# Tying a mixing's steps, two sets' copies and the casts at an entry to other rows of W

## The chip, the cores and the metric

The kernel runs on one core of one Trainium2 chip. The metric is the device time of one execution in microseconds; a kernel's time is the median of its timed runs. For the kernel before there are three: 2227.27, 2230.98 and 2233.45 us.

The core's engines run side by side, each through a queue of its own in order: TensorE (PE in the profile; PEld is its weight load), VectorE (DVE), ScalarE (ACT), GpSimd (POOL) and SyncE (SP), which issues transfers. ScalarE and GpSimd issue transfers too; those stand in their queues like any other instruction (ACTq, POOLq).

## The reference

Two layers on 512 tokens of 2048 channels, all in fp32. The first has an attention with forgetting and an RWKV part between the projections `ab_w_in` and `ab_w_out`. The second is a gMLP: `c_w_in` gives u, v and g, and the tokens are mixed in chunks of 128:

```
def chunked_spatial_gating(u, v, ln_g, ln_b, w_s, b_s):
    B, T, _ = v.shape
    u = jax.nn.gelu(u, approximate=False)
    v = layer_norm(jax.nn.gelu(v, approximate=False), ln_g, ln_b)
    vc = v.reshape(B, T // GMLP_CHUNK, GMLP_CHUNK, GMLP_GROUPS, GMLP_GROUP_CH)
    causal = jnp.tril(jnp.ones((GMLP_CHUNK, GMLP_CHUNK), w_s.dtype))
    mixed = jnp.einsum('gts,bnsgc->bntgc', w_s * causal, vc) + b_s.T[:, :, None]
    return u * mixed.reshape(B, T, GMLP_W)
...
        if i % 2 == 0:
            ...
            y = jnp.concatenate([oa * jax.nn.silu(ga), ob * jax.nn.silu(gb)], axis=-1) @ ab_w_out[j]
        else:
            proj = xn @ c_w_in[j]
            u, v, g = _split(proj, (GMLP_W, GMLP_W, GMLP_W))
            oc = chunked_spatial_gating(u, v, c_ln_g[j], c_ln_b[j], c_w_s[j], c_b_s[j])
            y = (oc * jax.nn.silu(g)) @ c_w_out[j]
        h = h + rms_norm(y, norm_post[i])
        h = h + (p[i] @ ple_w_proj[i]) * jax.nn.sigmoid(h @ ple_w_gate[i])
```

There are 16 mixing groups of 128 channels, each with its own 128 x 128 matrix.

## The kernel before

**Rows of W.** Each fp32 operand is split into a high part (ScalarE casts it to a rounded fp32, `whi`, L1544) and the rest (VectorE subtracts, `wlo`, L1545), and a product is three matmuls. The big products behind the first layer's gates (out projection, gate of the per-layer input, `c_w_in`, `c_w_out`, second gate) are each done by seven block products in place of eight (`seven`). Their weights come in pieces of 512 KB, two rows of 128 x 512 each; six of the eight piece buffers are `rq0` to `rq5`, two are `raw`. SyncE loads a piece (L1488), GpSimd's transfers (L1492) or VectorE (L1496) add a second block to it where a product needs a sum. For each row ScalarE casts, VectorE subtracts, and TensorE runs six matmuls of 512 columns, or twelve of 256 (L1580). Four `whi`/`wlo` buffers, and `half` at each fifth row, let the casts run about four rows ahead of TensorE.

**What sets the order.** Everything else is queued with `later(n, step)` on a clock that ticks once a row of W; a scheduler then lays the instructions into each engine's queue by priority, casts and subtracts of W first. `tc.issue_after(x)` binds an instruction to stand behind x in the queue of its engine; it adds no wait.

**The mixing.** In `layer_c`, `mix(g, at)` does one of the 16 groups, eight while the first half of u and g is computed and eight in the second. Its steps: load the saved v (`sq<-vd`, 256 KB, L1659), the group's matrix (L1660) and the two columns of the norm (L1661, L1662) over ScalarE's queue; normalise with four activations (L1668); mask the matrix on GpSimd (L1671); multiply and add the columns on VectorE (L1672, L1673); transpose the matrix on TensorE (L1678); split matrix and values (casts L1680 and L1683, subtracts L1681 and L1684); three matmuls (L1689 to L1691); and combine with u (L1693). The steps are queued at 11 and 4 rows ahead of `at`, at it, and 7 behind, with `at = 40 + int(6.8 * e)` for the e-th of eight.

**The sets.** A set is a block of the activations, or a sum of blocks, split into high and low parts by `finish` (cast L973, subtract L974). In `first_gate`, `early` makes the first set of the second layer and `x2` another.

**The entry.** In `layer_ab` the attention's last gate product is copied out of TensorE's accumulator, half by ScalarE (L2015) and half by VectorE (L2016), and the first rows of the out projection follow.

Of the kernel before, what the change touches and what calls it, by code (L numbers as in the profile page):

```python
# [16 lines left out]
P = 128  # L17
T = 512
# [88 lines left out]
class Net:  # L107
# [862 lines left out]
    def finish(self, src, hi, lo):  # L970

        nc = self.nc
        nc.scalar.copy(hi, src)  # L973
        nc.vector.tensor_tensor(lo, src, f(hi), ALU.subtract)  # L974

# [27 lines left out]
    def run(self):  # L1003
        tc = self.tc
        with ExitStack() as ctx:
# [14 lines left out]
            self.turns = 0  # L1020
            self.clock, self.todo = 0, []
# [7 lines left out]
    def rest(self, cp):  # L1029
        nc, tc, i = self.nc, self.tc, self.i  # L1030
        with ExitStack() as ctx:
# [5 lines left out]
            self.raws = deque([(self.wraw, "raw", 2)] * 2 + [(wq, f"rq{j}", 1) for j in range(6)])  # L1037
# [56 lines left out]
    def first_gate(self, H, state, wp, ps):  # L1094
# [38 lines left out]
        def early(q):  # L1133
            if q == 0:
                cs[1] = self.whole_set()
            self.put(cs[1], q, H[q, 0])

# [10 lines left out]
        steps += [(108 + q, lambda q=q: x2(q)) for q in range(4)]  # L1148
# [328 lines left out]
    def pieces(self, pr, prod, keep):  # L1477
# [20 lines left out]
        for j in range(4):  # L1498
# [36 lines left out]
            for a in range(2):  # L1535
# [5 lines left out]
                else:  # L1541
                    hi, lo = (self.t(self.wq, [P, T], f"half{x}", F32R) for x in range(2))
                with self.tc.high_priority(self.wpri):
                    self.cast = nc.scalar.copy(hi, src)  # L1544
                    nc.vector.tensor_tensor(lo, src, f(hi), ALU.subtract)  # L1545
# [70 lines left out]
    def layer_c(self, cp, sets, steps, accq, after, wp, ps):  # L1616
# [30 lines left out]
        def mix(g, at):  # L1647
# [6 lines left out]
            def load():  # L1654
                par = self.t(wp, [P, T], "accq", bufs=1) if g % 2 else self.rstdB
                own["ws"], own["bc"] = par[:, 0:P], par[:, P : 3 * P].rearrange("p (a c) -> p a c", c=P)
                vn = own["vn"] = self.t(wp, [P, 4, P], "sq")
                with tc.issue_after(self.cast.ins):
                    nc.scalar.dma_start(vn, self.vd[:, g])  # L1659
                nc.scalar.dma_start(own["ws"], i["c_w_s"][0, g])  # L1660
                nc.scalar.dma_start(own["bc"][:, 0, :], i["c_ln_g"][0, gs].partition_broadcast(P))  # L1661
                nc.scalar.dma_start(own["bc"][:, 1, :], i["c_ln_b"][0, gs].partition_broadcast(P))  # L1662

            def norm():
                ws, bc, vn = own["ws"], own["bc"], own["vn"]
                row = lambda j: bc[:, j : j + 1, :].broadcast_to([P, 4, P])
                for m in range(4):
                    nc.scalar.activation(  # L1668
                        vn[:, m, :], vn[:, m, :], AF.Identity, bias=nb[:, m : m + 1], scale=rv[:, m : m + 1]
                    )  # L1670
                nc.gpsimd.affine_select(ws, ws, [[-1, P]], ALU.is_ge, 0.0, 0, 1)  # L1671
                nc.vector.tensor_tensor(vn, vn, row(0), ALU.mult)  # L1672
                nc.vector.tensor_tensor(vn, vn, row(1), ALU.add)  # L1673

            def split():
                vn = own["vn"]
# [372 lines left out]
```

## Time and profile before

| | |
|---|---|
| timed runs | 2227.27, 2230.98, 2233.45 us |
| the profiled execution | 2223.7 us, its span 2222.0 us, mean granted clock 0.998 |
| TensorE busy | 2185.6 us, 98% |
| VectorE, ScalarE, GpSimd busy | 1659.4, 1353.2, 301.9 us |
| transfers | 343 MB, 155 GB/s on average |

The profile is of one execution. Times in its rows are microseconds from the span's start. A row of the timeline gives start, duration, engine, line, operation, what is written from what, the shape, and in brackets how long the engine had been idle and what ended that. A line that starts with an issuing queue (SPq, ACTq) is the issue of a transfer, not its duration. The end of a matmul is modelled, so a matmul ahead of a stop shows longer than it runs.

### The profile page before, as it was taken

Reading aid. Unit: us, or ns where it says so; the run is one execution under the profiler, and the core shown is the slowest. Engines: PE = TensorE matmul, PEld = TensorE weight load, DVE = VectorE, ACT = ScalarE, POOL = GpSimd, SP = SyncE. Lnnn points to the kernel's source line nnn. Section 1 sums busy time; section 2 is a strip of 40 time slices with the busy share of each in tenths; the row PEclk is TensorE's granted clock in tenths of the full one; section 3 lists DMA queues with packets and bytes.
Section 4 is the critical chain, followed back from the end, with each engine's and each line's share of the span. In section 5 each row is a group of like instructions: output and inputs, shape, how many; then the busy total and the mean of one; then the engine's idle time right before and its main releaser. Section 6 shows DMA issues by size and latency. Waiting matters only on the chain.

```text
span 2222.0 us, 43469 instructions
## 1 busy us (share of the span) xinstructions
PE 2185.6 (98%) x16535; PEld 1872.1 (84%) x16535; DVE 1659.4 (75%) x3228; ACT 1353.2 (61%) x2764; POOL 301.9 (14%) x360
## 2 busy tenths in 40 slices
PE   9999999999999999999999999999999999999998
PEld 7878888888888788889999999788877878999887
DVE  8756667657633778886979978987677678978977
ACT  5545545554543677775667766756655567657754
POOL 2001010101000000000210121110221221120031
PEclk9999999999999999999999999999999999999999
DMA  7322322223233633326797888787877887688796
GB/s 238 93 79 58 89 77 80 70 64 91 68 92 99 212 96 98 102 81 204 162 216 241 218 201 221 179 214 202 192 162 206 181 189 176 148 200 264 207 243 169
DMA packets 304144, 343.34 MB, mean 155 GB/s; under 512 B 15758, under 2 KB 187951, under 8 KB 302911
## 3 DMA queue, kind: packets, MB, share of 16 engines
q1 hardware_dynamic: 237438, 240.93, 34.6%
q0 software_dynamic: 44608, 85.99, 22.4%
q10 hardware_dynamic: 21888, 13.64, 2.1%
q8 instruction: 130, 2.13, 0.4%
q14 instruction: 80, 0.65, 0.1%
HBM read 305.61 MB, written 34.90 MB: 153 GB/s over the span
## 4 chain that ended last, share of the span: by engine, by line
PE 79%; DVE 8%; DMA 6%; ACT 4%; issue 2%; ACTq 0%; DVEq 0%; SPq 0%; POOLq 0%
PE mm L1580 37%; PE mm L213 10%; PE mm L215 9%; PE mm L214 9%; DMA sq<-vd 3%; DVE wlo L1545 2%; PE tm L551 1%; DMA rq<-in_ple_w_gate_dram 1%; PE tm L572 1%; ACT whi L1544 1%; PE g L923 1%; PE pp L340 1%; PE tm L484 1%; PE tm L910 1%; PE ch L636 1%
## 5 line engine op out<-in xcount | busy, mean ns | idle before, releaser
L1545 DVE TENSOR_TENSOR wlo<-rq,whi 128x512 fp32r<-128x512 f32 x485 | 329.7, 687 | 118.0 <-ACT whi L1544 115.6
L213 PE MATMUL mm<-xh,whi 128*128 128x512 f32 x992 | 411.7, 415 | 0.0
L1544 ACT CAST whi<-rq 128x512 fp32r<-128x512 f32 x485 | 297.4, 620 | 186.3 <-PE mm L1580 120.1
L215 PE MATMUL mm<-xh,wlo 128*128 128x512 f32 x992 | 391.7, 395 | 0.0
L214 PE MATMUL mm<-xl,whi 128*128 128x512 f32 x992 | 389.6, 393 | 0.0
L197 ACT CAST whi<-raw 128x512 fp32r<-128x512 f32 x272 | 167.5, 617 | 151.4 <-PE mm L214 107.8
L199 DVE TENSOR_TENSOR wlo<-raw,whi 128x512 fp32r<-128x512 f32 x272 | 185.9, 695 | 93.3 <-ACT whi L197 69.6
L215 PEld LDWEIGHTS mm<-xh,wlo 128*128 128x128 f32 x992 | 186.2, 188 | 41.2
L213 PEld LDWEIGHTS mm<-xh,whi 128*128 128x128 f32 x992 | 186.8, 188 | 33.2
L214 PEld LDWEIGHTS mm<-xl,whi 128*128 128x128 f32 x992 | 187.2, 189 | 29.8
L1580 PE MATMUL mm<-whi,yh 128*128 128x512 f32 x424 | 138.9, 394 | 5.1 <-ACT whi L1544 5.1
L1580 PE MATMUL mm<-whi,xl 128*128 128x512 f32 x424 | 137.5, 392 | 1.8 <-ACT whi L1544 0.9
L1580 PE MATMUL mm<-whi,yl 128*128 128x512 f32 x420 | 137.8, 394 | 0.0
L1544 ACT CAST whi<-raw 128x512 fp32r<-128x512 f32 x154 | 94.9, 620 | 69.0 <-PE mm L1580 48.5
L1545 DVE TENSOR_TENSOR wlo<-raw,whi 128x512 fp32r<-128x512 f32 x154 | 104.8, 687 | 39.6 <-ACT whi L1544 39.1
L1580 PE MATMUL mm<-xh,whi 128*128 128x256 f32 x696 | 126.9, 283 | 0.0
L1580 PEld LDWEIGHTS mm<-xh,whi 128*128 128x128 f32 x696 | 108.7, 192 | 0.1
L1492 POOL DMA_DIRECT2D rq<-in_c_w_in_dram x56 | 67.5, 1214 | 274.6 <-DVE wlo L1545 194.9
L1545 DVE TENSOR_TENSOR half<-rq,half 128x512 fp32r<-128x512 f32 x111 | 76.2, 686 | 36.8 <-ACT half L1544 36.6
L1580 PEld LDWEIGHTS mm<-whi,yh 128*128 128x128 f32 x424 | 80.3, 189 | 23.3 <-ACT whi L1544 6.8
L1580 PE MATMUL mm<-xh,wlo 128*128 128x256 f32 x348 | 98.5, 283 | 0.0
L1544 ACT CAST half<-rq 128x512 fp32r<-128x512 f32 x111 | 68.8, 620 | 46.0 <-PE mm L1580 26.9
(531 smaller groups left out, 5187.3 us busy)
## 6 DMA issues: line engine op xcount, KB each, us to landing
raw<-in_ab_w_in_dram SPq DMA_DIRECT2D x128, 512.0 KB, 3.9
rq<-in_c_w_in_dram POOLq DMA_DIRECT2D x56, 512.0 KB, 7.6
rq<-in_c_w_in_dram SPq DMA_DIRECT2D x50, 512.0 KB, 5.2
rq<-in_ple_w_gate_dram SPq DMA_DIRECT2D x44, 512.0 KB, 6.1
rq<-in_ple_w_gate_dram POOLq DMA_DIRECT2D x36, 512.0 KB, 9.4
raw<-in_c_w_in_dram SPq DMA_DIRECT2D x26, 512.0 KB, 7.4
rq<-in_c_w_out_dram SPq DMA_DIRECT2D x24, 512.0 KB, 4.7
rq<-in_ab_w_out_dram POOLq DMA_DIRECT2D x20, 512.0 KB, 7.5
```

Source lines behind the costliest of these rows:

```text
L197: nc.scalar.copy(hi[:, : m * n], src)
L199: self.weng.tensor_tensor(lo[:, : m * n], src, f(hi[:, : m * n]), ALU.subtract)
L213: nc.tensor.matmul(acc, hi, xhi[k], start=(k == 0), stop=False)
L214: nc.tensor.matmul(acc, hi, xlo[k], start=False, stop=False)
L215: nc.tensor.matmul(acc, lo, xhi[k], start=False, stop=(k == nk - 1))
L340: nc.tensor.matmul(acc, mat, part, start=(j == 0), stop=(j == 1))
L484: nc.tensor.matmul(pg[q][:, e], BK[pp, e].rearrange("p a t -> p (a t)"), AR[pp, e, q::2, :], start=True, stop=True)
L551: nc.tensor.matmul(px[dst, e, :], a[src, e, :], b[src, e, :], start=True, stop=True)
L1492: nc.gpsimd.dma_start(view(tl), block(*where), accum_op=ALU.add)
L1544: self.cast = nc.scalar.copy(hi, src)
L1545: nc.vector.tensor_tensor(lo, src, f(hi), ALU.subtract)
L1580: nc.tensor.matmul(o, x, y, start=(first and r == 0 and j == 0 and not a), stop=(r == 7 and j == 2), **more)
```

## The change

It has three parts, and the number of instructions of each kind stays as it was.

1. **Mixing.** Steps are cut smaller, and ScalarE's ones are bound by `row()` behind the latest cast of W: the two columns at 11 and 10 rows ahead of `at`, the matrix at 9, the load of v at 8, the mask and the transpose at 4 and 3; two activations of the norm at it, two more and the VectorE steps a row behind, the split at 3 rows and the matmuls at 4 rows behind. `at` becomes `42 + int(6.8 * e)`.
2. **Sets.** In `first_gate`, the casts of `early` and of `x2` are bound behind the latest cast of W.
3. **Entry.** The first piece of the out projection, `rq0`, gets a pool of its own that is opened early, and the third row's cast and subtract (the first of the second piece) are bound behind the two copies of the last gate product.

```diff
@@ -970,8 +970,12 @@
     def finish(self, src, hi, lo):
 
         nc = self.nc
-        nc.scalar.copy(hi, src)
+        with self.row() if self.tied else nullcontext():
+            nc.scalar.copy(hi, src)
         nc.vector.tensor_tensor(lo, src, f(hi), ALU.subtract)
+
+    def row(self):
+        return self.tc.issue_after(self.cast.ins)
 
     def gated(self, n, t, wp, tag, place):
 
@@ -1018,6 +1022,7 @@
             self.vd, self.yd2 = (self.t(dp, [P, c, 4, P], n) for n, c in (("vd", KT), ("yd2", 8)))
             self.homes = {}
             self.turns = 0
+            self.tied, self.entry = False, None
             self.clock, self.todo = 0, []
             self.ahead = {}
             self.weng = tc.nc.vector
@@ -1034,7 +1039,7 @@
             wp = pool("wp", 2)
             self.rstdB = self.t(cp, [P, T], "rstdB")
             wq = self.wq = pool("wq", 1)
-            self.raws = deque([(self.wraw, "raw", 2)] * 2 + [(wq, f"rq{j}", 1) for j in range(6)])
+            self.raws = deque([(self.wraw, "raw", 2)] * 2 + [(wq if j else self.wqa, f"rq{j}", 1) for j in range(6)])
             self.rp = pool("rp", 3)
             self.lpool = pool("lp", 1)
             h, scale = self.first_out(wp, ps)
@@ -1133,7 +1138,14 @@
         def early(q):
             if q == 0:
                 cs[1] = self.whole_set()
+            self.tied = True
             self.put(cs[1], q, H[q, 0])
+            self.tied = False
+
+        def second(q):
+            self.tied = True
+            x2(q)
+            self.tied = False
 
         steps = [((1, 6, 19, 28)[q], lambda q=q: late(q)) for q in range(4)]
         steps += [((11, 15, 32, 35)[q], lambda q=q: first(q)) for q in range(4)]
@@ -1145,7 +1157,7 @@
         steps += [(76, lambda: next_fetch(6, (6, 0), (7, 0)))]
         steps += [(90, lambda: fetch([self.slot("xl", k, F32) for k in range(4)], (6, 1), (7, 1), (4, 1), (5, 1)))]
         steps += [(103 + q, lambda q=q: early(q)) for q in range(4)]
-        steps += [(108 + q, lambda q=q: x2(q)) for q in range(4)]
+        steps += [(108 + q, lambda q=q: second(q)) for q in range(4)]
         for n, step in sorted(steps, key=lambda x: x[0]):
             self.later(n, step)
 
@@ -1540,9 +1552,13 @@
                     lo = self.t(self.wsp, [P, 512], "wlo", F32R)
                 else:
                     hi, lo = (self.t(self.wq, [P, T], f"half{x}", F32R) for x in range(2))
+                gates, self.entry = (self.entry if j else None), (None if j else self.entry)
+                behind = lambda x: self.tc.issue_after(gates[x]) if gates else nullcontext()
                 with self.tc.high_priority(self.wpri):
-                    self.cast = nc.scalar.copy(hi, src)
-                    nc.vector.tensor_tensor(lo, src, f(hi), ALU.subtract)
+                    with behind(0):
+                        self.cast = nc.scalar.copy(hi, src)
+                    with behind(1):
+                        nc.vector.tensor_tensor(lo, src, f(hi), ALU.subtract)
                 yield 2 * j + a, hi, lo
             if done is not None:
                 self.gone(done)
@@ -1652,35 +1668,50 @@
             own = {}
 
             def load():
-                par = self.t(wp, [P, T], "accq", bufs=1) if g % 2 else self.rstdB
-                own["ws"], own["bc"] = par[:, 0:P], par[:, P : 3 * P].rearrange("p (a c) -> p a c", c=P)
                 vn = own["vn"] = self.t(wp, [P, 4, P], "sq")
-                with tc.issue_after(self.cast.ins):
+                with self.row():
                     nc.scalar.dma_start(vn, self.vd[:, g])
-                nc.scalar.dma_start(own["ws"], i["c_w_s"][0, g])
-                nc.scalar.dma_start(own["bc"][:, 0, :], i["c_ln_g"][0, gs].partition_broadcast(P))
-                nc.scalar.dma_start(own["bc"][:, 1, :], i["c_ln_b"][0, gs].partition_broadcast(P))
-
-            def norm():
-                ws, bc, vn = own["ws"], own["bc"], own["vn"]
+
+            def column(j):
+                if j == 0:
+                    par = self.t(wp, [P, T], "accq", bufs=1) if g % 2 else self.rstdB
+                    own["ws"], own["bc"] = par[:, 0:P], par[:, P : 3 * P].rearrange("p (a c) -> p a c", c=P)
+                with self.row():
+                    nc.scalar.dma_start(own["bc"][:, j, :], i[("c_ln_g", "c_ln_b")[j]][0, gs].partition_broadcast(P))
+
+            def weights():
+                with self.row():
+                    nc.scalar.dma_start(own["ws"], i["c_w_s"][0, g])
+
+            def norm(ms):
+                vn = own["vn"]
+                with self.row():
+                    for m in ms:
+                        nc.scalar.activation(
+                            vn[:, m, :], vn[:, m, :], AF.Identity, bias=nb[:, m : m + 1], scale=rv[:, m : m + 1]
+                        )
+
+            def affine():
+                bc, vn = own["bc"], own["vn"]
                 row = lambda j: bc[:, j : j + 1, :].broadcast_to([P, 4, P])
-                for m in range(4):
-                    nc.scalar.activation(
-                        vn[:, m, :], vn[:, m, :], AF.Identity, bias=nb[:, m : m + 1], scale=rv[:, m : m + 1]
-                    )
-                nc.gpsimd.affine_select(ws, ws, [[-1, P]], ALU.is_ge, 0.0, 0, 1)
                 nc.vector.tensor_tensor(vn, vn, row(0), ALU.mult)
                 nc.vector.tensor_tensor(vn, vn, row(1), ALU.add)
 
+            def lower():
+                nc.gpsimd.affine_select(own["ws"], own["ws"], [[-1, P]], ALU.is_ge, 0.0, 0, 1)
+
+            def flip():
+                pw = own["pw"] = self.t(ps, [P, P], "mm")
+                nc.tensor.transpose(pw, own["ws"], self.ident)
+
             def split():
-                vn = own["vn"]
-                pw = self.t(ps, [P, P], "mm")
-                nc.tensor.transpose(pw, own["ws"], self.ident)
+                vn, pw = own["vn"], own["pw"]
                 w2 = own["w2"] = self.t(lp, [P, 2, P], "w2", F32R)
-                nc.scalar.copy(w2[:, 0], pw)
+                vh, vl = own["v"] = [self.t(wp, [P, 4, P], "sg", F32R) for _ in range(2)]
+                with self.row():
+                    nc.scalar.copy(w2[:, 0], pw)
+                    nc.scalar.copy(vh, vn)
                 nc.vector.tensor_tensor(w2[:, 1], pw, f(w2[:, 0]), ALU.subtract)
-                vh, vl = own["v"] = [self.t(wp, [P, 4, P], "sg", F32R) for _ in range(2)]
-                nc.scalar.copy(vh, vn)
                 nc.vector.tensor_tensor(vl, vn, f(vh), ALU.subtract)
 
             def mul():
@@ -1692,7 +1723,10 @@
                 ub = u[g // 4][:, :, g % 4 * P : g % 4 * P + P]
                 nc.vector.scalar_tensor_tensor(ub, pm, self.bsT[:, g : g + 1], ub, ALU.add, ALU.mult)
 
-            for n, step in ((-11, load), (-4, norm), (0, split), (7, mul)):
+            for n, step in (
+                (-11, lambda: column(0)), (-10, lambda: column(1)), (-9, weights), (-8, load),
+                (0, lambda: norm((0, 1))), (1, lambda: norm((2, 3))), (1, affine), (-4, lower), (-3, flip), (3, split), (4, mul),
+            ):
                 self.later(at + n, step)
 
         V = [Pair(W, D + 2 * j * T, 2 * j, vals) for j in range(2)]
@@ -1764,7 +1798,7 @@
             for j in range(2):
                 if step == nv + 14 * j + 1:
                     for e in range(8):
-                        mix(8 * j + e, 40 + int(6.8 * e))
+                        mix(8 * j + e, 42 + int(6.8 * e))
             if step == nv + 13:
                 for n in range(2):
                     self.later(4, lambda n=n: saved(n))
@@ -1971,7 +2005,7 @@
                 nc.vector.tensor_tensor(tl[oth], LO[own], f(tl[own]), ALU.subtract)
             self.rwkv_all(dense, first, rw, ps)
         self.weng = nc.vector
-        self.ya = pool("ya", 1)
+        self.ya, self.wqa = pool("ya", 1), pool("wqa", 1)
         for n in range(16):
             self.y[n] = self.slot("yl", n, F32)
             if n >= 8:
@@ -2012,8 +2046,8 @@
                 acc = dense(C_GATES[n])
                 gz[n] = self.t(fw, [P, T], "vT")
                 with tc.high_priority(2 * HP):
-                    nc.scalar.copy(gz[n][:, :256], acc[:, :256])
-                    nc.vector.tensor_copy(gz[n][:, 256:], acc[:, 256:])
+                    copies = nc.scalar.copy(gz[n][:, :256], acc[:, :256]), nc.vector.tensor_copy(gz[n][:, 256:], acc[:, 256:])
+                    self.entry = [x.ins for x in copies]
                 gate(n)
             self.weave([])
             gate(7)
```

ScalarE in the first mixing, around the load of the fifth group (its `sq`: sq_19878 before, sq_19944 after; `half` and `whi` are the casts of W). Before:

```order
L1544 CAST whi_19956<-rq_3904_19695 128x512
L1659 DMA sq_19878<-vd_103 128x512
L1544 CAST half_3967_19967<-rq_3913_19726 128x512
L1644 ACTIVATE mm_19638<-mm_19638,rc_17477 128x512
L1544 CAST whi_19990<-rq_3913_19726 128x512
L1668 ACTIVATE sq_19878<-sq_19878,nb_17481,rv_17480 128x128 x2
L1544 CAST whi_20008<-rq_3893_19639 128x512
L1683 CAST sg_19941<-sq_19770 128x512
L1680 CAST w_3960_19938<-mm_19936 128x128
L1668 ACTIVATE sq_19878<-sq_19878,nb_17481,rv_17480 128x128 x2
```

After:

```order
L1673 DMA sq_19944<-vd_103 128x512
L1607 COPY comb_19983<-mm_19872 128x512
L1559 CAST whi_20058<-rq_3900_19681 128x512
L1712 CAST w_3974_20001<-mm_19919 128x128
L1559 CAST whi_20070<-rq_3900_19681 128x512
```

Two instructions are left out here, a cast of the split and a column's load; then the same queue has

```order
L1559 CAST whi_20087<-rq_3910_19719 128x512
L1680 DMA accq_20009<-in_c_ln_b_dram 128x128
L1684 DMA accq_20009<-in_c_w_s_dram 128x128
L1673 DMA sq_20053<-vd_103 128x512
L1559 CAST whi_20098<-rq_3910_19719 128x512
L1690 ACTIVATE sq_19944<-sq_19944,nb_17484,rv_17483 128x128 x2
L1559 CAST half_4001_20119<-raw_19988 128x512
```

The load stood two casts ahead of the activations on it; now it stands four ahead. The load of the next group (sq_20053) stands between them, and the group's matrix (L1684) and columns (L1680) lie apart from it.

VectorE in the first layer's gate product, at the first of the four subtracts of `x2` (`yl_3368`; `half` and `wlo` are subtracts of W). Before:

```order
L1545 TENSOR_TENSOR wlo_16530<-rq_3183_16076,whi_16529 128x512
L1162 TENSOR_TENSOR accq_15682<-accq_15682,sq_16384 128x512
L1545 TENSOR_TENSOR wlo_16546<-rq_3183_16076,whi_16545 128x512
L1545 TENSOR_TENSOR wlo_16563<-rq_3188_16111,whi_16562 128x512
L974 TENSOR_TENSOR yl_3368_17362<-yh_2671_13221,yl_3367_17361 128x512
L1545 TENSOR_TENSOR half_3256_16579<-rq_3188_16111,half_3255_16578 128x512
L1545 TENSOR_TENSOR wlo_16596<-rq_3198_16158,whi_16595 128x512
```

After, at the place to which it and the three others went:

```order
L1561 TENSOR_TENSOR wlo_17333<-rq_3300_16889,whi_17332 128x512
L1561 TENSOR_TENSOR half_3366_17349<-rq_3300_16889,half_3365_17348 128x512
L975 TENSOR_TENSOR yl_3368_17365<-yh_2671_13224,yl_3367_17364 128x512
L1561 TENSOR_TENSOR wlo_17370<-rq_3305_16924,whi_17369 128x512
L1561 TENSOR_TENSOR wlo_17390<-rq_3305_16924,whi_17389 128x512
L1561 TENSOR_TENSOR wlo_17399<-rq_3310_16959,whi_17398 128x512
L975 TENSOR_TENSOR yl_3372_17386<-yh_2672_13228,yl_3371_17385 128x512
L975 TENSOR_TENSOR yl_3376_17394<-yh_2909_14657,yl_3375_17393 128x512
L1561 TENSOR_TENSOR wlo_17407<-rq_3310_16959,whi_17406 128x512
L975 TENSOR_TENSOR yl_3380_17403<-yh_2911_14664,yl_3379_17402 128x512
```

It stood behind the subtract of cast 179 of the casts by L1544, and stands behind that of cast 220 now.

VectorE at the entry (L2016, after it L2049, is the copy of the gate product). Before:

```order
L1545 TENSOR_TENSOR wlo_12774<-raw_12749,whi_12773 128x512
L1545 TENSOR_TENSOR wlo_12792<-raw_12789,whi_12791 128x512
L1545 TENSOR_TENSOR wlo_12808<-raw_12789,whi_12807 128x512
L2016 COPY vT_12716<-mm_12629 128x256
L1995 SCALAR_TENSOR_TENSOR yl_1649_9206<-vT_12716,yl_1649_9206 128x512
L1996 SCALAR_TENSOR_TENSOR yl_1649_9206<-th_12719,yl_1649_9206 128x512
L1996 SCALAR_TENSOR_TENSOR yl_1654_9211<-th_12723,yl_1654_9211 128x512
```

After:

```order
L1561 TENSOR_TENSOR wlo_12777<-raw_12752,whi_12776 128x512
L2049 COPY vT_12719<-mm_12632 128x256
L2029 SCALAR_TENSOR_TENSOR yl_1649_9209<-vT_12719,yl_1649_9209 128x512
L1561 TENSOR_TENSOR wlo_12795<-raw_12792,whi_12794 128x512
L1561 TENSOR_TENSOR wlo_12811<-raw_12792,whi_12810 128x512
L2030 SCALAR_TENSOR_TENSOR yl_1649_9209<-th_12722,yl_1649_9209 128x512
L1561 TENSOR_TENSOR wlo_12851<-rq_2597_12832,whi_12850 128x512
```

The copy moved ahead of two subtracts of W, those of the second piece of the out projection (raw_12789, now raw_12792), and the first subtract of `rq0` follows soon behind.

## The prediction

> **What bounds the kernel now.** I read the page first, then the waits, then the busy time by stretches, then the timeline at the three places where TensorE stops. The page's busy times and its chain say where the time is:
>
> ```profile
> PE 2185.6 (98%) x16535; PEld 1872.1 (84%) x16535; DVE 1659.4 (75%) x3228; ACT 1353.2 (61%) x2764; POOL 301.9 (14%) x360
> PE 79%; DVE 8%; DMA 6%; ACT 4%; issue 2%; ACTq 0%; DVEq 0%; SPq 0%; POOLq 0%
> ```
>
> TensorE sets the end, and no edit here takes a matmul away. So all that can be won is time in which TensorE waits or runs slowly. The 98% hides that: the ends of matmuls are modelled, and the last one before a stop looks longer than it is. I therefore count matmuls per stretch as well. The waits name two transfers that sit in front of casts and subtracts:
>
> ```profile
> ACT sq L1668 <- DMA sq<-vd: 49.6, 15, 6.8
> DVE yl L974 <- DMA hd<-yl: 14.3, 3, 8.0
> ```
>
> (total us, times, longest.) The first is the mixing's load of v: ScalarE's first normalisation stands in the queue until it lands, and all casts of W stand behind that. Now the stretches (us, then busy PE, PEld, DVE, ACT, POOL with counts, granted clock, DMA share, GB/s):
>
> ```profile
> 1360.00:1440.00 80.00, 78.42 (x377) 64.77 (x377) 72.52 (x116) 56.73 (x104) 13.06 (x12) 1.00 0.74 186
> 1600.00:1692.00 92.00, 86.83 (x370) 68.60 (x369) 68.67 (x113) 55.35 (x109) 20.03 (x21) 0.98 0.76 185
> 1692.00:1760.00 68.00, 68.00 (x302) 56.33 (x301) 47.44 (x70) 40.54 (x68) 13.28 (x12) 1.00 0.82 184
> 1760.00:1850.00 90.00, 85.73 (x376) 66.67 (x375) 64.95 (x107) 57.41 (x117) 18.67 (x18) 1.00 0.79 190
> ```
>
> 1692 to 1760 is undisturbed and all 512 wide: 68.00 / 302 = 0.225 us a matmul, so a row of W (6 of them) is about 1.36 us. 1600 to 1692 holds most of the first eight mixing groups: 370 matmuls, 8 of them 128 wide (one transpose a group; half a wide one, 0.11 us, is my estimate). Undisturbed they need 362 x 0.225 + 8 x 0.11 = 82.4 us; 9.6 us are lost. 1760 to 1850 holds most of the other eight, with 31 narrow ones: 345 x 0.225 + 31 x 0.11 = 81.1 us; 8.9 us are lost. **The two mixings lose 18.5 us.** The largest stop shows how:
>
> ```profile
> 1662.44 0.33 ACTq L1659 DMA_DIRECT2D sq<-vd  x1
> 1662.82 0.62 ACT L1544 CAST whi<-rq 128x512 fp32r<-128x512 f32 x1 [0.84 <-DVE sg L1684]
> 1663.40 0.62 ACT L1544 CAST half<-rq 128x512 fp32r<-128x512 f32 x1
> 1670.83 0.49 ACT L1668 ACTIVATE sq<-sq,nb,rv 128x128 f32<-128x128 f32 x1 [6.81 <-DMA sq<-vd]
> 1672.63 0.69 DVE L1545 TENSOR_TENSOR wlo<-rq,whi 128x512 fp32r<-128x512 f32 x1 [7.20 <-ACT whi L1544]
> 1672.65 0.77 PE L1580 MATMUL mm<-whi,yh 128*128 128x512 f32 x1 [3.22 <-ACT whi L1544]
> 1670.00:1680.00 10.00, 7.35 (x25) 5.63 (x26) 7.37 (x13) 7.83 (x16) 0.28 (x1) 0.83 0.65 169
> ```
>
> The load is issued at 1662.44, two casts ahead of its use; it takes 8.4 us; ScalarE stands 6.81 us, and TensorE 3.22 us. The difference, 3.6 us, is the cover: the rows that are already cast and subtracted. Behind the stop the clock is granted at 0.83 for 10 us, which is 1.7 us more.
>
> **The change part by part.** The counts of instructions stay as they are on every engine, so only places are priced.
>
> *Mixing.* The load now stands 8, 8, 6, 8, 4, 6, 8 and 6 casts ahead of its first use in each set of eight groups, where it was 2 or 3. In rows of 1.36 us that is 5.4 to 10.9 us. How long the loads take:
>
> ```profile
> DMA to landing us min/median/max: 2.7/5.5/9.0
> ```
>
> So the median load lands inside every distance but one, where it is 0.1 us late, and the longest (9.0) is late by 3.6 us at the distance of four and by 0.8 at six: not above the cover of 3.6. The ties also add waits. The load's issue now stands on ScalarE behind its cast and waits until VectorE's L1684 of an earlier group has released the sq buffer; behind it queue the next casts, for which VectorE and then TensorE wait. And TensorE's three mixing matmuls now use a split whose cast stands up to four rows ahead of the row that TensorE is at, which is the newest there can be; before, five or more rows had been cast since. The steps on that path, one of each kind:
>
> ```profile
> L1683 ACT CAST sg<-sq 128x512 fp32r<-128x512 f32 x7 | 4.3, 621 | 0.1
> L1684 DVE TENSOR_TENSOR sg<-sq,sg 128x512 fp32r<-128x512 f32 x7 | 4.8, 681 | 0.0
> L1681 DVE TENSOR_TENSOR w<-mm,w 128x128 fp32r<-128x128 f32 x8 | 2.3, 282 | 0.0
> L1673 DVE TENSOR_TENSOR sq<-sq,rstdB 128x512 f32<-128x512 f32 x3 | 2.1, 686 | 0.0
> ```
>
> L1673, then the cast, then L1681 and L1684: 0.69 + 0.62 + 0.28 + 0.68 = 2.27 us. That is the upper bound of a new wait per group, if this chain begins only when TensorE arrives; the lower bound is nothing. Six of the sixteen groups have the cast four rows ahead, and there L1673 stands a cast or more before it, so that a row of matmuls (1.36 us) covers over half: 2.27 - 1.36 = 0.9 us for six, and hardly anything for ten, makes about 0.3 us a group. The stretch 1360 to 1440 bears on the rest: VectorE is busy 72.52 of 80 us there, more than the mixings will be (68.67 of 82.4), and TensorE idles 1.58 us only. I take 0.25 us a group, 4 us in all, as what stays. **Gain 18.5 - 4 = 14.5 us**; the bounds are 18.5 and 18.5 - 16 x 2.27 = -17.8 us.
>
> A rule of the Trainium skill speaks against this term. "DMA: Bandwidth & Descriptors", in its section on the anatomy of a DMA, fits about 2.0 us and the bytes at 436 GB/s to a transfer (measured on GpSimd's path); for the load's 256 KB that is an estimate of 2.6 us. By it the old two casts (2.7 us) would do, the tie would gain nothing, and the sum would be 5 us instead of 19.5. The trace has 2.7 us as the minimum and 5.5 as the median, so the fit holds here for a quiet queue only, and the measurement decides.
>
> *The copies of two sets for the second layer.* One subtract of x2 stood on VectorE, early, behind a save of the buffer it overwrites:
>
> ```profile
> 1289.67 0.37 SPq L1164 DMA_DIRECT2D hd<-yl  x1
> 1300.88 0.69 DVE L974 TENSOR_TENSOR yl<-yh,yl 128x512 fp32r<-128x512 f32 x1 [8.02 <-DMA hd<-yl]
> 1302.23 1.46 PE L1580 MATMUL mm<-xh,half 128*128 128x256 f32 x10 [3.30 <-DVE half L1545]
> ```
>
> That save lands 11 us after its issue, and TensorE stops for 3.30 us. The copy is now behind cast 220, some forty rows later, where nothing of that save is outstanding. What is late next there: casts 220 to 224 share ScalarE with eight copies, 13 x 0.52 us (the step from a cast at 1011.45 to the copy behind it at 1011.97, quoted below) = 6.8 us, in five rows of 1.36, 6.8 us. It just fits and the cover is whole, so I price it at 0.3; if the cover is gone it costs up to four copies, 2 us. **Gain 3.0 us** (1.3 to 3.3).
>
> *The entry to the first out projection.*
>
> ```profile
> 1011.45 0.62 ACT L1544 CAST whi<-raw 128x512 fp32r<-128x512 f32 x1 [2.10 <-PE mm L214]
> 1011.97 0.37 ACT L2015 COPY vT<-mm 128x256 f32<-128x256 f32 x1
> 1012.10 0.69 DVE L1545 TENSOR_TENSOR wlo<-raw,whi 128x512 fp32r<-128x512 f32 x1 [2.02 <-ACT whi L1544]
> 1012.82 0.42 DVE L2016 COPY vT<-mm 128x256 f32<-128x256 f32 x1
> 1011.25 0.39 PE L215 MATMUL mm<-xh,wlo 128*128 128x512 f32 x1
> 1013.30 0.51 PE L1580 MATMUL mm<-yh,whi 128*128 128x256 f32 x2 [1.66 <-DVE vT L2016]
> 1015.45 3.32 SPq L1488 DMA_DIRECT2D rq<-in_ab_w_out_dram  x6
> 1019.56 0.62 ACT L1544 CAST half<-rq 128x512 fp32r<-128x512 f32 x1 [1.52 <-DMA rq<-in_ab_w_out_dram]
> 1020.27 1.90 PE L1580 MATMUL mm<-yh,half 128*128 128x256 f32 x12 [0.96 <-issue]
> ```
>
> TensorE waits for VectorE's half of the gate copy, which stands behind a subtract that nobody needs yet. The matmul before ends at 1011.64; the copy may run then, 0.42 us, and TensorE starts near 1012.1 instead of 1013.30: 1.2 us. The third and fourth rows' casts and subtracts come behind it and are needed two rows later. The second stop is the piece in rq0, which is issued only at 1015.45; now it is loaded far ahead. Of its 0.96 us I keep 0.8, because the next piece is still issued near 1015 and 4 us of landing (1015.45 to 1019.5) leave it little room. The early load stands in SyncE's queue near 740 us, ahead of loads of W_in, and carries a wait for one reload from DRAM issued before it. If that held the queue for a landing (5.5 us, as the loads of v take), and the rows in hand covered 3.6 of it, it would cost 1.9; I take none, since the reload is ahead of it in the same queue by several issues. **Gain 2.0 us** (0 to 2.2).
>
> Sum: 14.5 + 3.0 + 2.0 = 19.5 us. The profiled execution (2223.7 us, span 2222.0) becomes 2204. The median of the timed runs is 2230.98, 7.3 above the profiled one; on it the sum gives **2211.5 us**.
>
> **The rivals.** *The loads come late still.* For it: the DMA engines are busy 0.76 to 0.79 in the two stretches, and with the same bytes in 10% less time it is about 0.85. If the loads at distances four and six then take as long as the one of 8.4 us, and meet a VectorE that is behind, the mixing keeps half of its 18.5 and 2 of what stays anyway: 7 + 3 + 2 = 12, time 2219. Against it: the distance of eight, which half the groups have, is above the longest load.
>
> *The loads are not what costs.* TensorE's stops in the mixing may be VectorE's backlog, and the waits for vd lie in its shadow. For it speaks a stop with VectorE named:
>
> ```profile
> 1629.79 0.50 PE L1580 MATMUL mm<-wlo,yl 128*128 128x512 f32 x1 [0.58 <-DVE wlo L1545]
> ```
>
> Against it: VectorE is busy 68.67 of 92 us. Then only the other two edits count, 5 us: 2226, no change that can be measured. By the page's fit above the time would be the same.
>
> *TensorE waits for the mixing's own casts* (slower). At L1689 and L1690, from the order: the mixing matmuls now stand up to four rows closer to their operands. Each group pays up to the 2.27 us chain; 23.5 us (18.5 + 3 + 2) is what all edits free, so it decides from 23.5 / 16 = 1.47 us a group, and at the full price the time is 2231 - 23.5 + 36.3 = 2244. Against it: ten groups have the cast fewer than four rows ahead.
>
> *The change does not do what it says*: the order of the instructions shows the moves, so this needs no chance of its own.
>
> **How the numbers follow.** The forecast (2205 to 2217) has 0.60, late loads (2217 to 2224) 0.20, loads that do not count (2224 to 2238) 0.12, the slower case 0.08. About 0.3% (6.7 us) is what a measurement of this kernel can tell from no change, so faster is 0.80, the same 0.12, slower 0.08. The range 2203 to 2227 holds the first two and part of the third; the lower end is the forecast with the mixing's loss gone nearly whole.
>
> **What would show it right or wrong.** Right: the wait of sq for vd falls from 49.6 us to under 10; the two mixing stretches shrink by about 7 us each, with no stop over 1 us and a clock of 1.00; no subtract waits 8 us for hd; the first out matmul follows the last gate matmul by 0.9 us instead of 2.05. Wrong: stops of TensorE at the mixing matmuls, named to sg; or the vd waits as large as before; or VectorE's subtracts end last in both mixings at the same total loss.

## The result and the profile after

The change takes 2210.49 us (median of four runs, 2206.33 to 2215.19) where the kernel before takes 2231.28: a ratio of 0.9909 (0.9885 to 0.9934). Run again beside its parts it takes 2211.16 us against 2224.87, a ratio of 0.9937 (0.9925 to 0.9949), from 5 and 19 runs. So it gains 14 to 21 us, and the smaller figure is the one with the narrower interval. What differs between the two is the kernel before, at 2231 us and then at 2225; the change stayed near 2211. Its profiled execution, at 2215.19 us, is the slowest of the first four.

The page and the waits of the change, in the order of those before:

```profile
PE 2184.2 (99%) x16535; PEld 1875.3 (85%) x16535; DVE 1663.0 (75%) x3228; ACT 1356.6 (61%) x2764; POOL 299.7 (14%) x360
PE 83%; DVE 6%; DMA 4%; issue 4%; ACT 3%; SPq 0%; ACTq 0%; POOL 0%; DVEq 0%; POOLq 0%
...
ACT sq L1690 <- DMA sq<-vd: 8.9, 3, 5.8
```

ScalarE's wait for v fell from 49.6 us to 8.9. VectorE's wait for hd<-yl is gone from the list. The stretches of the two mixings tell more (columns as before):

```profile
1600.00:1692.00 92.00, 86.73 (x372) 69.78 (x371) 71.73 (x115) 59.06 (x116) 18.27 (x19) 0.96 0.75 175
1675.00:1690.00 15.00, 14.83 (x54) 11.71 (x55) 9.87 (x16) 6.99 (x14) 0.00 (x0) 0.82 0.48 139
1760.00:1840.00 80.00, 79.99 (x365) 64.88 (x365) 65.80 (x106) 58.40 (x116) 18.73 (x19) 1.00 0.87 209
```

By the same count of matmuls, the second half lost 80 - (334 x 0.225 + 31 x 0.11) = 1.4 us instead of 8.9. But the first half lost 92 - (364 x 0.225 + 8 x 0.11) = 9.2 us, against 9.6 before. Seven of its eight groups now cost little, and one stop has most of it. The timeline, on ScalarE, GpSimd and TensorE:

```profile
1658.77 1.00 ACTq L1673 DMA_DIRECT2D sq<-vd  x1
1667.26 0.62 ACT L1559 CAST whi<-raw 128x512 fp32r<-128x512 f32 x1 [0.72 <-PE mm L1596]
1673.74 0.88 ACT L1690 ACTIVATE sq<-sq,nb,rv 128x128 f32<-128x128 f32 x2 [5.85 <-DMA sq<-vd]
1674.52 0.60 ACT L1713 CAST sg<-sq 128x512 fp32r<-128x512 f32 x1
1675.17 0.80 PE L1720 MATMUL mm<-sg,w 128*128 128x512 f32 x1 [5.27 <-ACT sg L1713]
...
1673.30 0.28 POOL L1701 TENSOR_SCALAR_AFFINE_SELECT accq<-accq 128x128 f32<-128x128 f32 x1 [16.31 <-DMA accq<-in_c_w_s_dram]
```

The load of v for the eighth group is issued six casts ahead, as planned, and lands 15 us later. Behind the activations that wait for it stands the cast of the seventh group's values (L1713), and TensorE waits for that one. So the stop joins two of the rivals: a load that comes late, and a mixing matmul that waits for its own cast. The granted clock of 0.82 in the 15 us behind it is another 2.7 us, so this one stop costs 8.0 of the 9.2 us.

The entry got worse (ScalarE, then TensorE; the last two rows are stretches):

```profile
1022.48 1.14 ACT L1559 CAST whi<-rq 128x512 fp32r<-128x512 f32 x2 [3.09 <-DMA rq<-in_ab_w_out_dram]
1011.84 0.50 PE L1596 MATMUL mm<-yh,whi 128*128 128x256 f32 x2 [0.92 <-DVE vT L2049]
1023.15 0.50 PE L1596 MATMUL mm<-yh,whi 128*128 128x256 f32 x2 [2.43 <-ACT whi L1559]
1020.00:1025.00 5.00, 2.35 (x18) 1.94 (x17) 1.98 (x5) 2.52 (x5) 0.00 (x0) 0.99 0.95 341
1025.00:1035.00 10.00, 10.00 (x73) 10.00 (x73) 7.59 (x15) 6.03 (x11) 4.55 (x4) 0.83 0.99 245
```

The first out matmul starts 0.74 us sooner, as 0.92 stands for 1.66. But the next piece is waited for 2.43 us instead of 0.96, and then the clock is 0.83 for 10 us, which is 1.7 us more.

### The profile page after: what moved, and what is told of

Read it like the earlier page. It is cut to its first block, busy times and chain, and to the rows that moved or that the text cites. A ratio compares the mean times of both kernels' runs of the same rounds, so it can differ in the third digit from the quotient of the medians.

```text
span 2213.5 us, 43467 instructions
## 1 busy us (share of the span) xinstructions
PE 2184.2 (99%) x16535; PEld 1875.3 (85%) x16535; DVE 1663.0 (75%) x3228; ACT 1356.6 (61%) x2764; POOL 299.7 (14%) x360
## 4 chain that ended last, share of the span: by engine, by line
PE 83%; DVE 6%; DMA 4%; issue 4%; ACT 3%; SPq 0%; ACTq 0%; POOL 0%; DVEq 0%; POOLq 0%
PE mm L1596 43%; PE mm L213 9%; PE mm L215 9%; PE mm L214 9%; DVE wlo L1561 2%; PE tm L551 1%; DMA rq<-in_ple_w_gate_dram 1%; PE tm L572 1%; PE g L923 1%; DMA sq<-vd 1%; PE tm L484 1%; PE tm L910 1%; PE pp L340 1%; ACT whi L197 1%; PE ch L636 1%
## 5 line engine op out<-in xcount | busy, mean ns | idle before, releaser
L1596 PE MATMUL mm<-xl,whi 128*128 128x256 f32 x520 | 95.5, 284 | 0.1
L1596 PEld LDWEIGHTS mm<-whi,xl 128*128 128x128 f32 x424 | 79.6, 188 | 18.2 <-DVE xl L975 0.9
```

Of the source, the lines that this page charges most:

```text
L1596: nc.tensor.matmul(o, x, y, start=(first and r == 0 and j == 0 and not a), stop=(r == 7 and j == 2), **more)
```

## The experiments

All times are medians. The kernels ran in three groups of four, in the order of the table; each group ran on one chip, and each on a different one, beside runs of the kernel before. The kernel before took 2224.87 us in the first group, 2225.62 in the second and 2226.41 in the third. Ratios of different groups can be compared, the times less well.

| Kernel | us | ratio to before (95%) |
|---|---|---|
| the change again | 2211.16 | 0.9937 (0.9925 to 0.9949) |
| mixing alone | 2215.54 | 0.9956 (0.9945 to 0.9968) |
| sets alone | 2219.62 | 0.9975 (0.9965 to 0.9986) |
| entry alone | 2228.13 | 1.0012 (1.0003 to 1.0020) |
| change, no early piece | 2213.88 | 0.9952 (0.9939 to 0.9966) |
| change, no tie at the entry | 2207.85 | 0.9921 (0.9908 to 0.9935) |
| no early piece, last group later | 2207.76 | 0.9927 (0.9913 to 0.9941) |
| no early piece, matrix earlier | 2215.43 | 0.9959 (0.9944 to 0.9974) |
| change, no tie, again | 2208.42 | 0.9919 (0.9903 to 0.9935) |
| change, tie at the fourth row | 2209.61 | 0.9925 (0.9909 to 0.9941) |
| no tie, last group later from its mask | 2200.40 | 0.9878 (0.9861 to 0.9895) |
| no tie, load at two rows | 2216.41 | 0.9954 (0.9939 to 0.9969) |

### The three parts

The change as a whole:

> The changed kernel once more, beside its parts. Theory A (the terms of the prediction add): 19.5 us below the kernel before, 15 to 25. Theory B (the profiled execution of the change, 8.5 us below the profiled one of before, is the typical one): 6 to 12 us below. In the profile: theory A has no stop of over 1 us at the last group of the first mixing; theory B has the stop of 5.3 us again, with a load of v of about 15 us.

The mixing alone, without the ties of the sets and without the entry's part (the first two lines stand for two places each; the early pool goes too):

```diff
-            self.tied = True
+            self.tied = False
-            self.raws = deque([(self.wraw, "raw", 2)] * 2 + [(wq if j else self.wqa, f"rq{j}", 1) for j in range(6)])
+            self.raws = deque([(self.wraw, "raw", 2)] * 2 + [(wq, f"rq{j}", 1) for j in range(6)])
-                    self.entry = [x.ins for x in copies]
```

> The mixing's part alone (copies of the two sets and the entry as before). Theory A: 14.5 us below the kernel before (11 to 18). Theory B: 7 us below, since the first eight groups lose as much as before (9.4 us against 9.9) and only the second eight gain. By both, the stops for the first out piece (about 1 us) and for hd<-yl (3.3 us) are there as before.

The sets alone (the mixing's code and the entry as before, the two ties kept):

> The ties of the copies of the two sets alone. Theory A: 3.0 us below the kernel before (1 to 4), the 8 us wait of VectorE for hd<-yl gone. Rival (the stop was hidden by what comes next, since the second layer's pieces are late anyway): no change, within 1 us.

The entry alone (the mixing's code as before, `self.tied = False`):

> The entry's part alone: rq0's early load, and the third row's cast and subtract behind the last copies. Theory A: 2.0 us below the kernel before (0 to 2.2). Theory B (the profile of the change: 1.1 us instead of 1.8 at the copy, but 2.6 us instead of 1.1 at the next piece, which lands 6.8 us after its issue): 1 us above the kernel before (0 to 3), with a stop for rq<-in_ab_w_out of over 2 us.

From the ratios, the mixing gains 9.8 us (0.0044 x 2224.87), the sets gain 5.6 and the entry loses 2.7. Together that is 12.7 us, and the change gains 14.0. So the parts add within the intervals. But the 14.0 lies between the ranges of the two theories (15 to 25 and 6 to 12), and so does the mixing's 9.8 (11 to 18, and 7). The sets gave more than the 1 to 4 us expected, and the entry lost, as its theory B had it. The load of the eighth group took 13.7 us in the mixing alone and in the change again (rows of ScalarE, first the mixing alone, then the change again):

```profile
1658.66 1.49 ACTq L1673 DMA_DIRECT2D sq<-vd  x1
1672.32 0.88 ACT L1690 ACTIVATE sq<-sq,nb,rv 128x128 f32<-128x128 f32 x2 [4.56 <-DMA sq<-vd]
```

```profile
1659.48 1.39 ACTq L1673 DMA_DIRECT2D sq<-vd  x1
1673.21 0.88 ACT L1690 ACTIVATE sq<-sq,nb,rv 128x128 f32<-128x128 f32 x2 [4.93 <-DMA sq<-vd]
```

So that stop is no chance of one execution; there theory B was right, and theory A's sign (no stop over 1 us at the last group) failed. What the sets gain is more than the 3.3 us stop of the profile before. In the mixing alone, where the old place of the subtract is still in use, the stop and the stretch behind it read:

```profile
1299.15 0.69 DVE L975 TENSOR_TENSOR yl<-yh,yl 128x512 fp32r<-128x512 f32 x1 [8.81 <-DMA hd<-yl]
1300.49 1.86 PE L1596 MATMUL mm<-xh,half 128*128 128x256 f32 x7 [5.18 <-DVE half L1561]
1300.00:1310.00 10.00, 9.51 (x58) 9.51 (x59) 6.73 (x10) 2.48 (x4) 0.00 (x0) 0.68 0.77 232
```

The stop is 5.18 us, and the clock behind it 0.68. The entry alone shows the same (4.66 us and 0.73). The profile before had caught a mild case, 3.30 us with no slower clock:

```profile
1302.00:1312.00 10.00, 9.77 (x81) 9.77 (x82) 9.12 (x14) 3.72 (x6) 0.00 (x0) 1.00 0.85 240
```

How often the kernel before itself has the longer stop is not shown, as only one execution of it was profiled.

### The two halves of the entry

The change without the early load of rq0, by the edit of `self.raws` above:

> The change without the early load of rq0 (its tie of the third row's cast and subtract kept). Theory A (the early piece is what costs at the entry: it lets TensorE run through the first piece and stop longer at the second, and that stop takes the clock down): 3 to 4 us faster than the change, 17 us below the kernel before; the stop at the out projection's third piece row is 1 to 2 us and the clock there 1.00. Theory B (the tie costs): within 1 us of the change.

The change without the tie of the third row (`self.entry` is never set):

> The change without the tie of the third row's cast and subtract (rq0 loaded early). Theory A: no faster than the change, up to 1 us slower, the stop of over 2 us and the lower clock stay or grow less than 1 us smaller. Theory B (the tie costs): 3 to 4 us faster than the change.

My theory of that moment, that the early piece costs, fell: without it the kernel is no faster (0.9952 against 0.9937, the intervals overlap). Without the tie it is 3.6 us faster than the change (0.9921 against 0.9937, from two groups, and the intervals overlap), and the repeat gave 0.9919. TensorE's first waits, without the early piece and then without the tie (the repeat):

```profile
1009.49 0.50 PE L1596 MATMUL mm<-yh,whi 128*128 128x256 f32 x2 [0.92 <-DVE vT L2049]
1019.15 2.76 PE L1596 MATMUL mm<-yh,half 128*128 128x256 f32 x12 [3.65 <-issue]
```

```profile
1010.22 0.51 PE L1596 MATMUL mm<-yh,whi 128*128 128x256 f32 x2 [1.66 <-DVE vT L2049]
```

With the early piece and no tie the second stop is gone, in both executions. With the tie and no early piece it is 3.65 us, with a clock of 0.70 over the 5 us from 1020. The stops bear the times out: at the entry the change loses 0.92 + 2.43 us and 1.7 us in clock, the kernel without the tie 1.66 us, so 3.4 us less; the kernel before loses 1.66 + 0.96 us, so 2.4 us less than the change, where the entry alone was measured 2.7 us slower. What the tie moves is seen on VectorE and on SyncE's queue; the change first, then the repeat without the tie:

```profile
1011.36 0.42 DVE L2049 COPY vT<-mm 128x256 f32<-128x256 f32 x1 [4.72 <-ACT vT L2049]
1012.42 1.29 DVE L1561 TENSOR_TENSOR wlo<-raw,whi 128x512 fp32r<-128x512 f32 x2
1013.74 0.37 SPq L1500 DMA_DIRECT2D raw<-in_ab_w_out_dram  x1
1014.83 0.69 DVE L2030 SCALAR_TENSOR_TENSOR yl<-th,yl 128x512 f32<-128x512 f32 x1
1015.62 9.21 SPq L1500 DMA_DIRECT2D rq<-in_ab_w_out_dram  x7
```

```profile
1009.02 0.69 DVE L1561 TENSOR_TENSOR wlo<-raw,whi 128x512 fp32r<-128x512 f32 x1 [2.02 <-ACT whi L1559]
1009.74 0.42 DVE L2049 COPY vT<-mm 128x256 f32<-128x256 f32 x1
1011.00 1.29 DVE L2030 SCALAR_TENSOR_TENSOR yl<-th,yl 128x512 f32<-128x512 f32 x2
1012.38 7.61 SPq L1500 DMA_DIRECT2D rq<-in_ab_w_out_dram  x7
```

The subtracts of the third and fourth rows are the last readers of a raw buffer. In the change they end at 1013.7, and the next raw load is issued then, 1.88 us ahead of the pieces. Without the tie they ended earlier, and from the same timeline the raw load goes out 2.64 us ahead of the pieces. The gate's last step (L2030), whose end releases the pieces, also moved back by 0.9 us against the last gate matmul. The first piece in the burst of seven takes 1022.48 - 1015.62 = 6.9 us in the change, from its issue to the cast that waits for it. In the repeat without the tie it takes 5.3 us at most, as its cast waited for TensorE and not for the piece; in the first run without the tie, where the cast did wait for it, it took 4.6.

The change with the tie at the fourth row:

```diff
-                gates, self.entry = (self.entry if j else None), (None if j else self.entry)
+                gates, self.entry = (self.entry if j and a else None), (None if j and a else self.entry)
```

> The change with the tie one row later: the fourth row's cast and subtract stand behind the last copies, the third row's ahead of them as before. Theory A (the tie costs because the subtract of the third and fourth rows also frees the raw buffer, so that the next load of W comes 1.6 us later and runs into the pieces behind the gate, which land 2 us later): the raw load is issued about 2.0 us after the last gate matmul instead of 3.2, the stop at the second piece falls under 1 us, and the time is 3 to 5 us below the change. Rival (any work put behind the copies delays the gate's last step and so the pieces): the stop of over 2 us stays and the time is within 1.5 us of the change.

It is 0.9925, between the change and the kernel without the tie, and not to be told from either. SyncE, ScalarE and TensorE's second stop:

```profile
1013.71 9.34 SPq L1500 DMA_DIRECT2D rq<-in_ab_w_out_dram  x7
1020.71 1.14 ACT L1559 CAST whi<-rq 128x512 fp32r<-128x512 f32 x2 [3.21 <-DMA rq<-in_ab_w_out_dram]
1021.38 0.51 PE L1596 MATMUL mm<-yh,whi 128*128 128x256 f32 x2 [1.35 <-ACT whi L1559]
```

Here the pieces are issued no later than without a tie, only the raw load is still late (2.6 us behind the last gate matmul instead of 1.6), and the first piece still takes 7.0 us. That speaks for the collision with the raw load as the larger part. Other executions agree: with the raw load 2.6 us ahead of the pieces the first one takes 4.1 us (the kernel before) and 4.6, and with 1.3 to 1.9 us ahead it takes 5.8 to 7.0. The stop was 1.35 us, with the clock at 1.00, where I expected under 1. Of the change's 2.43 us, an estimate from these rows gives 0.9 to the later issue of the pieces and about 1.5 to the longer landing; no run separates the two.

### The mixing's last group, and the distance

Without the early piece, and the eighth group of the first half three rows later from its norm on:

```diff
-                self.later(at + n, step)
+                self.later(at + n + (3 if g == 7 and n >= 0 else 0), step)
```

> Without the early piece, and the norm and what follows it of the first half's last mixing group three rows later, its load as before: so the split of the group before stands ahead of that norm in ScalarE's queue. Theory A (the stop of 4 to 5 us at the matmuls of the seventh group is that group's cast standing behind the next group's norm, which waits for a load of about 15 us): 4 to 6 us faster than without the early piece alone. Rival (the late load only moves the stop to the eighth group): within 1.5 us, a stop of 3 us or more at the eighth group.

It is 5.6 us faster than without the early piece alone (0.9927 against 0.9952). The cast of the seventh group goes ahead of the waiting norm, and the stop of 5.2 us is gone. A smaller one came in its place, at the transpose of the eighth group's matrix. It is the stop of 3 us or more that the rival named, though the time came out as in theory A:

```profile
1670.91 0.33 PE L1705 MATMUL mm<-ident,accq 128*128 128x128 f32 x1 [3.18 <-POOL accq L1701]
1670.57 0.28 POOL L1701 TENSOR_SCALAR_AFFINE_SELECT accq<-accq 128x128 f32<-128x128 f32 x1 [16.46 <-DMA accq<-in_c_w_s_dram]
```

The eighth group's matrix is late as v is. Without the early piece, with each group's matrix loaded at 14 rows ahead instead of 9, masked at 2 instead of 4 and transposed at 1 instead of 3 (its buffer is taken with the matrix then):

```diff
-                (-11, lambda: column(0)), (-10, lambda: column(1)), (-9, weights), (-8, load),
-                ... (1, affine), (-4, lower), (-3, flip), ...
+                (-11, lambda: column(0)), (-10, lambda: column(1)), (-14, weights), (-8, load),
+                ... (1, affine), (-2, lower), (-1, flip), ...
```

> Without the early piece, and each group's matrix loaded five rows earlier and masked two rows later. Theory A (GpSimd's mask waits up to 16 us for the matrix, the accumulating transfers of W behind it bunch up, and that bunch makes the last load of v late): GpSimd's waits in the masks fall from about 120 us to under 40, the load of v for the eighth group lands in under 10 us, and the time is 3 to 6 us below the one without the early piece alone. Rival (the stretch has too many transfers whatever their order): the load is still at 13 us or more, and the time is within 1.5 us.

No gain in time (0.9959 against 0.9952). In its profile the stop in the first half is 1.22 us instead of 5.18, and the eighth group's load of v took 11.2 us (1659.02 to 1670.20): neither the under 10 of theory A nor the 13 or more of the rival. But the second half has a new stop at the mixing matmuls. First the stop of the first half, then the new one:

```profile
1671.26 0.50 PE L1719 MATMUL mm<-sg,w 128*128 128x512 f32 x1 [1.22 <-ACT sg L1712]
1814.18 0.50 PE L1719 MATMUL mm<-sg,w 128*128 128x512 f32 x1 [2.12 <-ACT sg L1712]
```

GpSimd's waits at the masks were 92 us, by the count that gives 120 without this edit, and not under 40. So whether GpSimd's bunched transfers make the load late stays open: the order did matter, but this edit moved more than the bunch.

The change without the tie at the entry, once more, as the base of the last two:

> The change without the tie of the third row again, as the base of the next three: 4 us below the change, 16 to 18 us below the kernel before.

On it, the eighth group three rows later from its mask on (`n > -8` in place of `n >= 0` above):

> The change without the tie of the third row, and the eighth mixing group of the first half three rows later from its mask on, its loads as before. Both findings add: 4 to 6 us below the change without the tie, 21 to 24 us below the kernel before; in the profile no stop over 3 us in the first mixing.

2200.40 us, 8 us below its base and 26 below the kernel before, where 4 to 6 and 21 to 24 were expected; the fastest here. The base stops 4.49 us at the seventh group's values, and its clock of 0.96 over the 90 us from 1600 is another 3.6 us, so 8.1 us together. The first mixing now has no stop:

```profile
1590.00:1680.00 90.00, 90.00 (x400) 73.25 (x399) 76.60 (x124) 62.69 (x123) 21.24 (x22) 1.00 0.80 191
```

And the change without the tie, with the load of v at two rows ahead instead of eight:

> The change without the tie of the third row, but the load of v at two rows ahead of the norm instead of eight, all other steps of the mixing cut and tied as in the change. Theory A (the distance of the load is what gains in the mixing): 7 to 12 us above the change without the tie, ScalarE's wait of sq for vd back at 40 us or more. Rival (the cutting and tying of the other steps gains): within 2 us of it.

It is 8 us slower than its base (0.9954 against 0.9919). ScalarE's wait for v is back, though at 24.5 us and not at the 40 or more that I expected. TensorE again stops behind the norm (4.11 us in the first half) and at mixing matmuls (up to 2.41 us); one of them stands here:

```profile
ACT sq L1690 <- DMA sq<-vd: 24.5, 8, 8.2
1777.27 0.50 PE L1720 MATMUL mm<-sg,w 128*128 128x512 f32 x1 [1.22 <-ACT sg L1713]
```

So the distance of the load is the larger part of the mixing's gain of 9.8 us. That the cutting and tying of the other steps gives the remaining 2 us is a difference of two groups of runs, smaller than their intervals.

## Why the prediction came out

The time was inside the range and within 1 us of the forecast (2210.49 against 2211.5 us), but that closeness is luck. The gain was forecast as 19.5 us, and the better measurement gives 14.0 (11.3 to 16.7). The forecast took it off a kernel before at 2230.98 us, which ran some 5 us faster in all three later groups, and the two errors cancel. The direction of the whole and the mechanism of two parts were right; the sizes of all three were not.

*Mixing: 14.5 forecast, 9.8 measured.* The mechanism held: seven of eight groups in the first half and all in the second nearly stopped costing. What I left over, 4 us, was spread as 0.25 us a group; the profile has 9.2 + 1.4 = 10.6 us left, and 8.0 of it in one group. The step that failed is "the longest (9.0) is late by 3.6 us at the distance of four and by 0.8 at six: not above the cover of 3.6". It took the longest landing of before as a bound. The load at distance six took 13.7 to 15.0 us in this stretch, and in the profile of the change it was 5.85 us late. Both rivals spoke of this, each of one half: the loads come late, and TensorE waits for the mixing's own cast. Neither said that one queue joins them, as the seventh group's cast stood behind the eighth group's norm. When that order was turned and the mask moved too, 8 us came free, so without that stop the term would come to about 9.8 + 8 = 18 us, above the 14.5; that is an estimate across two groups of runs.

*Sets: 3.0 forecast, 5.6 measured.* The mechanism was right: the 8 us wait is gone and no new one came at casts 220 to 224. The term was sized by a stop of 3.30 us with no slower clock. Two other kernels with the old order stop there for 4.66 and 5.18 us and then run at a clock of 0.73 and 0.68. So the size was most likely off because the profile before had a mild case, which is argued and not shown.

*Entry: gain of 2.0 forecast, loss of 2.7 measured.* The copy's 1.2 us came as 0.74. The failed step is "the third and fourth rows' casts and subtracts come behind it and are needed two rows later". I asked when their results are needed, and not what their end releases: a raw buffer, and with it the next load of W, which then runs into the pieces. I also kept 0.8 us of the second stop with a landing of 4 us, for a piece that is one of seven issued together; it took 6.9. The early piece without the tie does gain: TensorE then has no second stop, which was 0.96 us before.

*What would have shown it.* Two of the four signs came: the vd wait under 10 us and no 8 us wait for hd. The third came in part, as the first out matmul follows the last gate matmul by 1.3 us, nearer than 2.05 but not 0.9. The fourth, no stop over 1 us in the mixings and 7 us less in each, came in the second half (8.9 to 1.4 us) and failed in the first.

The sum had no term of its own for what a stop costs in clock. In these traces a stop of 3.30 us kept the clock at 1.00, and one of 3.22 us brought 0.83 over the next 10 us. The stop of 2.43 us at the entry brought 0.83 too, and one of 2.05 us there, in the change run again, 0.86. The Trainium skill, "TensorE: Matmul & The Clock Gate", in its part on the clock gate, has the clock halve after an idle window of about 3.4 us, in windows that run free of the kernel. The traces agree in part, as two stops of nearly one length (3.22 and 3.30 us) came out differently. But those of 2.05 and 2.43 us are shorter than the window, and there the measurement decides: a stop of 2.4 us can cost another 1.7 us in clock.

## What to carry to other kernels

When a step is moved behind another, list what its end releases, not only who needs its result: a buffer's last reader sets when the next load goes out, and what that load then meets. A wait removed by issuing a transfer earlier is gone only where the transfer can land in that distance under the load of that stretch; the longest landing seen before is no bound for a new place. And in a queue that runs in order, the steps of one item should stand ahead of the next item's step that waits for a transfer.

## What the runs showed that I had not expected

- A load of 256 KB took 13.7 to 15.0 us at one place of the program, in execution after execution, where before it took 9.0 at most anywhere. Around it the transfer engines are busy 1.06 and 0.99 of the time (the first two rows). The share alone does not explain it: before, the load at this place took 8.4 us at 0.91 (the last row). The cause stays open:

```profile
1650.00:1660.00 10.00, 10.00 (x47) 8.18 (x46) 7.84 (x13) 6.28 (x13) 4.40 (x5) 1.00 1.06 202
1660.00:1675.00 15.00, 9.90 (x44) 7.83 (x42) 8.36 (x15) 7.45 (x16) 0.28 (x1) 0.95 0.99 267
1660.00:1675.00 15.00, 11.78 (x46) 8.59 (x45) 7.80 (x14) 7.35 (x16) 2.97 (x4) 0.92 0.91 206
```

- The same stop, after the same wait, cost 3.30 us with no slower clock in one execution and 5.18 us with a clock of 0.68 in another. From 1000 us on, the fourteen traces here have thirteen stops of TensorE of 3.65 us or more, and the granted clock over the next 5 us was 0.50 to 0.69 behind every one. Of nine stops between 2.05 and 3.30 us, seven were followed by 0.66 to 0.71 and two (3.18 and 3.30 us) by 1.00. So in that range the length of a stop does not tell its price.
